# A Hymba-style layer on one core: weight-sum stores, out-projection loads and the first loads put on other queues, and four token rows of the prompt split behind a weight block

## The chip, the cores and the metric

The kernel runs on one core of a Trainium2 chip. The metric is the device time of one launch in microseconds (us); lower is better. 0.2% of the time before is 4.2 us.

## The reference

One encoder layer, called for two inputs that share all weights: a prompt of 512 tokens and a sample of 1024 tokens, model width 2048. All values are fp32.

```
h = rms_norm(x, norm_g)
z = h @ w_in                                  # 2048 -> 5632
c_val, c_glu, c_gate, q, k, v, a_gate = split(z)
conv = conformer_conv(c_val, c_glu, ...)      # sigmoid gate, 31-tap depthwise conv, layer norm, silu, @ w_pw
att  = banded_sink_attention(rope(q), rope(k), v, sink)   # 8 heads, 2 kv heads, window 128
mix  = concat(conv * silu(c_gate), att * silu(a_gate)) @ w_out
y    = rms_norm(x + mix, final_norm_g)
```

## The kernel before

**Products.** TensorE (PE) multiplies in a rounded fp32 form (`fp32r`), so every fp32 operand is split into a high part `hi` and the remainder `lo`, and a product is three matmuls: hi·hi, hi·lo and lo·hi. The split is `parts()` (line 510): ACT writes `hi` with a Copy, DVE writes `lo = x - hi`. Token rows are split by the same function with the norm gain as scale (lines 514 and 515). A token row `t1_n` is 128 model channels by 512 tokens; a weight tile `hl_n` holds both parts of a block.

**Units.** The sample's in- and out-projection run in a seven-product block scheme (class `Unit`): a unit covers a 2x2 grid of weight blocks, and its seven products P1, P2, P6, P5, P7, P3, P4 have 12 matmuls of 128x128 by 128x512 each (line 207). The weights of a unit come as two raw tiles `r1` and `r2` (loads in lines 123 and 127, ring of 3 raw tiles), from which `make0` to `make3` build the split weight tiles `hl` (ring of 3). `make1` forms the differences of blocks that P5, P6 and P4 need, and `less2` the one of P7 (line 143). In the out-projection of the sample (`w_out`), where `sums` is set, these four differences of a unit are also stored to DRAM as `wsum_P..`, because the prompt's out-projection uses them again: 16 units with 4 stores of 256 KB each, made of 512 rows of 512 bytes. The stores are made by `e.store` (line 504), that is, on SyncE's queue (SP).

**The out-projection's accumulators.** Units of class `Onto` do the out-projection in two halves of the contraction. The first half, `over[0]`, starts each of the four output quarters of a unit from the residual `xT_s`, and stores the partial results as `part_out..`; the second half, `over[1]`, starts from `part_out..` and writes the result `y_d`. A quarter lives in an accumulator tile (`u_n` or `g_n`, rings of four), which `begin()` loads (line 285) and into which DVE adds every product when it is done (line 304). `begin()` is called `ahead` products before the quarter's first product, by default two; `u.ahead = 0` is set for the first two units of the second half. These two run as a pair, product by product in turns, since their weights and tokens (`mix_d`, loaded as `p_n` on SP in line 878 and split into `t1_n`) become ready together. The code order sets the order of each queue, up to what the tile scheduler moves by priority; a queue works strictly in order, and a DMA whose tile is not free or not yet written holds what stands behind it.

**The partial sums of the in-projection.** On GpSimd's queue (POOL) stand the stores of partial in-projection results (`part_q`, `part_conv`, `part_gate`, `part_kv`, line 268) and the loads that add them from DRAM into a tile (line 501, an accumulating DMA). POOL has no DMA in the out-projection.

**The prompt's start.** The prompt's in-projection (matmuls in line 669) begins right behind the last unit of the sample's, called `end`. While `end` runs, the prompt's 16 token rows are loaded and split, four behind each of `end`'s first four products (`end.after[0]` to `end.after[3]`, function `follow`), and the first weight block of the prompt is split behind them. The last four token rows (12 to 15) come in with the two loads `load_two(12)` and `load_two(14)`.

**The head.** SP first loads the norm gain `norm_g`, then the first weight block and the sample's token rows in turns (`first()`, line 1888). PE meanwhile runs 20 dummy matmuls of 128x128 by 128x128 (`warm`, line 559).

Of the kernel before, what the change touches and what calls it, by code (L numbers as in the profile page):

```python
# [7 lines left out]
F32 = mybir.dt.float32  # L8
# [5 lines left out]
P = 128  # L14
D = 2048
ND = D // P
# [17 lines left out]
W = 512  # L34
# [59 lines left out]
class Unit:  # L94
# [50 lines left out]
    def make1(self):  # L145

        if self.late:
            t2 = self.e.G([HALF, P]) if self.side or not self.total else self.e.A([HALF, P], F32)
        else:
            t2 = self.e.PT("p", NP, [HALF, P])  # L150
        r1, r2 = self.r1, self.r2
        self.sub(r1[:, 0], r2[:, 0], r1[:, 0])
        self.sub(t2, r2[:, 1], r1[:, 0])
        self.sub(r1[:, 1], r1[:, 1], t2)
        if self.sums:
            for name, x in (("P5", r1[:, 0]), ("P6", t2), ("P4", r1[:, 1])):
                self.e.store(self.sums[name], x)
        t = self.e.hl_tile()
        for o, x in enumerate((r1[:, 0], t2)):
            self.e.parts(t[:, 0, o], t[:, 1, o], x)  # L160
        return t

    def less2(self):
        self.sub(self.r2[:, 0], self.r2[:, 1], self.r2[:, 0])
        if self.sums:
            self.e.store(self.sums["P7"], self.r2[:, 0])
        self.lessened = True

    def make2(self):
# [261 lines left out]
class Encoder:  # L431
# [74 lines left out]
    def parts(self, hi, lo, x, g=None):  # L506

        nc = self.nc
        if g is None:
            nc.scalar.activation(hi, x, AF.Copy)  # L510
            nc.vector.tensor_tensor(lo, x, hi.bitcast(F32), ALU.subtract)  # L511
            self.low_made = nc.cur_bb.bb.instructions[-1]
        else:
            nc.scalar.activation(hi, x, AF.Identity, scale=g)
            nc.vector.scalar_tensor_tensor(lo, x, g, hi.bitcast(F32), ALU.mult, ALU.subtract)
# [45 lines left out]
    def constants(self):  # L561
        nc, a = self.nc, self.a

        def load(key, shape):
            t = self.const.tile([P] + shape, F32, name="c_" + key)
            nc.sync.dma_start(t, a[key])
            return t

        self.norm_g = load("norm_g", [ND])
        self.ones = self.const.tile([P, P], F32, name="ones")  # L570
        nc.vector.memset(self.ones, 1.0)
        self.ones_r = self.const.tile([P, P], F32R, name="ones_r")
        nc.vector.tensor_copy(self.ones_r, self.ones)
        self.norm_n = self.const.tile([P, ND], F32, name="norm_n")

        def rest():
            self.ident = load("ident", [P])
            self.mask = load("mask", [3 * P])
            self.w_dw = load("w_dw", [NC, TAPS])
            self.b_dw = load("b_dw", [NC])  # L580
            self.w_both = self.const.tile([P, NC, (TAPS + 1) // 2], F32, name="w_both")
            nc.vector.tensor_copy(self.w_both[:, :, TAPS // 2 :], self.w_dw[:, :, TAPS - 1 :])
            nc.vector.tensor_tensor(
                self.w_both[:, :, : TAPS // 2], self.w_dw[:, :, 0 : TAPS - 1 : 2], self.w_dw[:, :, 1 : TAPS - 1 : 2], ALU.add
            )
            self.ln_g = load("conv_ln_g", [NC])
            self.ln_b = load("conv_ln_b", [NC])
            self.sink = load("attn_sink", [HEADS])
            self.fin_g = load("final_norm_g", [ND])
            self.stat = {s: self.const.tile([P, TS // P], F32, name=f"stat{s}") for s in (0, 1)}  # L590

        self.more_constants = rest
# [132 lines left out]
    def spread(self, cols, b=NB, room=None):  # L725

        nc = self.nc
        hi = self.work.tile([P, b], F32R, tag="tinyr", bufs=4, name=self.name("tinyr"))
        lo = self.small(b)
        nc.vector.tensor_copy(hi, cols)  # L730
        nc.vector.tensor_tensor(lo, cols, hi.bitcast(F32), ALU.subtract)
        parts = []
        for part in (hi.bitcast(F32), lo):
            dg = (room or self.U)([b * P], F32R)
            for j in range(b):
                nc.vector.tensor_scalar(dg[:, j * P : (j + 1) * P], self.ident, part[:, j : j + 1], None, ALU.mult)
            parts.append(dg)
        yield S8
        ps = self.PS("s", [b * P])
        for n, dg in enumerate(parts):  # L740
            nc.tensor.matmul(ps, self.ones_r, dg, start=n == 0, stop=n == 1)
        return ps
# [1115 lines left out]
def encoder(ctx, tc, a):  # L1858
    e = Encoder(ctx, tc, a)
    sample, prompt = Sequence(e, 0), Sequence(e, 1)  # L1860
# [24 lines left out]

    def first():
        x = [e.F([TS]) for _ in range(NF)] + [e.A([TS], F32)]
        part = lambda k, t: e.nc.sync.dma_start(x[k][:, t * W : t * W + W], sample.xT[k][:, t * W : t * W + W])
        plain.begin()
        for k in range(2 * HALF):  # L1890
            half, j = divmod(k, HALF)
            if j == 0:
                plain.load_some(0, half, 0, 1)
            part(k, 0)
            if j == 0:
                plain.load_some(1, half, 0, 1)
                plain.load_some(0, half, 1)
            if j == 1:
                plain.load_some(1, half, 1)
        for k in range(2 * HALF):  # L1900
            part(k, 1)
        e.loaded = 2
        e.w_load(3)
        e.warm(20, True)
        sums = sample.first_sums(x)
        x = None
        for half in range(2):
            for j in range(HALF):
                if j == 0:
                    plain.make_some(0, half, 0, 1)  # L1910
                next(sums)
                if j < 2:
                    plain.make_some(1 - j, half, j, HALF if j else 1)
                if j == 1:
                    plain.make_some(1, half, 1)
        e.nc.vector.tensor_scalar(e.norm_n, e.norm_g, -1.0, None, ALU.mult)
        for k in range(2 * HALF):
            next(sums)
        e.ready = 2
        plain.after[3] = [lambda: next(sums)]  # L1920
        plain.after[5] = [lambda: e.T.pop("A21")]
        second = stages[0][2]
        for step in (0, 2, 3):
            second.after.setdefault(step, []).append(lambda: next(sums, None))
        second.after[4] = [e.more_constants]
        second.after.setdefault(6, []).append(lambda: setattr(e, "calm", False))

    for u in stages[0][1:3]:
        u.order = TURNS
    plain.before.append(first)  # L1930

    def switch(unit, nxt, g, seq):
# [58 lines left out]
    def load_two(j):  # L1991
        if 8 <= j < 12:
            for i in (0, 1):
                xp[j + i] = e.PT("p", NP, [W])
                e.nc.sync.dma_start(xp[j + i], prompt.xr_d[j // 2][:, i])
            return
        t = e.A([2, TP], F32)
        e.nc.sync.dma_start(t, prompt.xr_d[j // 2])
        xp[j], xp[j + 1] = t[:, 0], t[:, 1]

    def follow(step):
        for k in range(4 * step, 4 * step + 4):
            prompt.split(k, xp.pop(k))
        if step == 0:
            load_two(12)
            load_two(14)
# [6 lines left out]
    end = stages[3][-1]  # L2013
    end.look = NHL - 1
    end.before.append(last_before)
    for step in range(4):
        end.after[step] = [lambda step=step: follow(step)]

    pj = prompt.jobs()
    pj[0].behind = pj[0].early = True  # L2020
# [65 lines left out]
        u.next = v  # L2086
    jobs += grouped(over[0], None) + grouped(over[1], e.A)
    for u in over[1][:2]:
        u.ahead = 0
    over[1][0].next = None  # L2090
    fj[-1].before.append(lambda: chain[0].begin((0, 0)))

# [67 lines left out]
```

## Time and profile before

| | |
|---|---|
| Time, 3 runs | median 2084.76 us (2084.57 to 2086.94) |
| Profiled execution | 2080.18 us, of it 2078.4 us span |
| Granted PE clock, mean | 0.997 of full speed |
| PE busy | 2060.7 us (99%), 9259 matmuls |
| DVE busy | 1754.4 us (84%) |
| ACT busy | 1043.6 us (50%) |
| POOL busy | 122.6 us (6%) |
| DMA | 494.55 MB, mean 238 GB/s |

PE is busy for 99% of the span, so what can change is what lies in the rest: the places where PE waits, and those where its clock was granted only in part. Times within the profile are counted from the start of the span. A row of the timeline gives the start, the time until the last of its instructions ends, the engine (SPq, ACTq and POOLq are a queue's DMA issues), the line, the operation, its tiles, the count, and in brackets how long the engine stood idle before and for what.

### The profile page before, as it was taken

The page shows a single profiled execution, that of the slowest core. Times are in us where ns is not written, and L with a number is a line of the kernel's source. Part 1 is how long each engine was busy: PE and PEld are TensorE (multiplying, and loading weights), DVE is VectorE, ACT ScalarE, POOL GpSimd, SP SyncE. Part 2 cuts the span into 40 slices and gives each one's busy share as a digit, 9 for nine tenths or more (in the row PEclk, how much of TensorE's full clock was granted, in tenths as well). Part 3 has the DMA queues.
Part 4 walks back from the last instruction along what each step waited for, and adds up shares of the span by engine and source line. Part 5 has one row for each costly group of instructions (what it writes and reads, how often), then busy time and mean ns, then how long its engine had stood idle before and what let it go on. Part 6 is the DMA issues. An engine that isn't in the chain of part 4 may idle for free.

```text
span 2078.4 us, 27092 instructions
## 1 busy us (share of the span) xinstructions
PE 2060.7 (99%) x9259; PEld 1699.2 (82%) x9259; DVE 1754.4 (84%) x2873; ACT 1043.6 (50%) x1711; POOL 122.6 (6%) x176
## 2 busy tenths in 40 slices
PE   9999999999999999999999999999999999999998
PEld 8888888888888888788888888888888887888886
DVE  8767899998899999999666877767799977998887
ACT  7485445333464434554455777336454343454454
POOL 0111111111111111100000000000000000000000
PEclk9999999999999999999999999999999999999999
DMA  8888886864577767954455555996789899678897
GB/s 288 312 298 256 199 223 221 285 220 160 188 242 192 175 169 183 280 166 156 153 172 187 177 182 183 315 330 234 247 289 300 278 299 293 220 247 298 289 333 277
DMA packets 245819, 494.55 MB, mean 238 GB/s; under 512 B 23600, under 2 KB 84400, under 8 KB 245680
## 3 DMA queue, kind: packets, MB, share of 16 engines
q1 hardware_dynamic: 225136, 445.62, 63.9%
q0 software_dynamic: 19392, 45.10, 9.4%
q10 hardware_dynamic: 1152, 2.10, 0.3%
q8 instruction: 72, 1.18, 0.2%
q14 instruction: 67, 0.55, 0.1%
HBM read 331.77 MB, written 160.96 MB: 237 GB/s over the span
## 4 chain that ended last, share of the span: by engine, by line
PE 48%; DVE 7%; issue 6%; DMA 4%; ACT 2%; POOL 1%; SPq 0%; ACTq 0%; POOLq 0%; DVEq 0%
PE a L669 13%; PE a L207 7%; PE c L669 6%; PE b L669 6%; PE c L207 3%; PE pv L1196 2%; PE a L1835 2%; PE s L1167 2%; PE s L1835 2%; PE b L207 1%; PE pt L1201 1%; DVE hl L511 1%; DVE f L1003 1%; DVE t L511 1%; DVE f L1040 1%
## 5 line engine op out<-in xcount | busy, mean ns | idle before, releaser
L207 PE MATMUL a<-t,hl 128*128 128x512 f32 x2640 | 633.6, 391 | 4.7 <-DVE u L304 3.2
L207 PEld LDWEIGHTS a<-t,hl 128*128 128x128 f32 x2640 | 494.7, 188 | 110.6 <-DVE u L304 3.6
L510 ACT ACTIVATE hl<-raw 128x1024 fp32r<-128x1024 f32 (+3 forms) x334 | 296.1, 890 | 384.5 <-PE c L207 81.6
L511 DVE TENSOR_TENSOR hl<-raw,hl 128x1024 fp32r<-128x1024 f32 (+3 forms) x334 | 338.8, 1015 | 145.8 <-ACT hl L510 144.4
L669 PE MATMUL a<-t,hl 128*128 128x512 f32 x1344 | 328.0, 394 | 0.0
L207 PE MATMUL c<-t,hl 128*128 128x512 f32 x1320 | 319.2, 389 | 0.0
L207 PEld LDWEIGHTS c<-t,hl 128*128 128x128 f32 x1320 | 247.3, 188 | 51.6 <-DVE u L304 0.4
L669 PEld LDWEIGHTS a<-t,hl 128*128 128x128 f32 x1344 | 248.6, 188 | 49.8
L1040 DVE SCALAR_TENSOR_TENSOR f<-f,c_w_dw,f 128x512 f32<-128x512 f32 x248 | 173.9, 750 | 0.3
L669 PE MATMUL b<-t,hl 128*128 128x512 f32 x672 | 164.6, 395 | 2.2 <-DVE hl L511 2.2
L1003 DVE SCALAR_TENSOR_TENSOR f<-f,c_w_dw,f 128x512 f32<-128x512 f32 x232 | 163.7, 748 | 1.2 <-ACT f L998 1.2
L669 PE MATMUL c<-t,hl 128*128 128x512 f32 x672 | 164.2, 393 | 0.3 <-DVE hl L511 0.3
L207 PE MATMUL b<-t,hl 128*128 128x512 f32 x660 | 160.0, 389 | 0.0
L669 PEld LDWEIGHTS b<-t,hl 128*128 128x128 f32 x672 | 126.1, 190 | 28.0 <-DVE hl L511 2.6
L669 PEld LDWEIGHTS c<-t,hl 128*128 128x128 f32 x672 | 124.7, 188 | 25.5 <-DVE hl L511 0.7
L207 PEld LDWEIGHTS b<-t,hl 128*128 128x128 f32 x660 | 123.7, 188 | 25.6
L1032 DVE SCALAR_TENSOR_TENSOR f<-f,w_both,f 128x512 f32<-128x512 f32 x120 | 90.0, 750 | 2.1
L236 ACT ACTIVATE u<-a 128x512 f32<-128x512 f32 x82 | 48.7, 594 | 66.8 <-PE a L207 64.2
L236 ACT ACTIVATE g<-a 128x512 f32<-128x512 f32 x78 | 46.3, 594 | 69.1 <-PE a L207 64.6
L1181 ACT ACTIVATE p<-p,tiny 128x384 f32<-128x384 f32 (+1 forms) x96 | 54.5, 570 | 39.8 <-DVE tiny L1178 27.3
L510 ACT ACTIVATE a<-pt 128x512 fp32r<-128x512 f32 x64 | 37.9, 593 | 66.3 <-PE pt L1201 66.2
L511 DVE TENSOR_TENSOR a<-pt,a 128x512 fp32r<-128x512 f32 x64 | 44.1, 689 | 27.3 <-ACT a L510 26.6
(350 smaller groups left out, 2687.9 us busy)
## 6 DMA issues: line engine op xcount, KB each, us to landing
raw<-w_in SPq DMA_DIRECT2D x170, 512.0 KB, 5.3
raw<-w_out SPq DMA_DIRECT2D x31, 512.0 KB, 5.0
raw<-w_pw SPq DMA_DIRECT2D x24, 512.0 KB, 4.2
wsum_P<-raw SPq DMA_DIRECT2D x47, 256.0 KB, 3.3
raw<-wsum_P SPq DMA_DIRECT2D x18, 512.0 KB, 5.0
f<-x_s SPq DMA_DIRECT2D x16, 512.0 KB, 8.2
g<-wsum_P SPq DMA_DIRECT2D x28, 256.0 KB, 4.2
a<-sum_S SPq DMA_DIRECT2D x24, 256.0 KB, 6.2
```

What stands on the lines that cost most here:

```text
L207: nc.tensor.matmul(acc, hl[:, l, o, j, :], toks[j][:, r], start=name in FRESH and j == 0 and q == 0, stop=name in LAST and j == HALF - 1 a ...
L236: nc.scalar.activation(t, bank, AF.Copy)
L510: nc.scalar.activation(hi, x, AF.Copy)
L511: nc.vector.tensor_tensor(lo, x, hi.bitcast(F32), ALU.subtract)
L669: nc.tensor.matmul(job.acc[0], hl[:, l, kk // HALF, kk % HALF, :], r, start=i == 0 and p == 0, stop=i == nk - 1 and p == 2,)
L1003: nc.vector.scalar_tensor_tensor(t, h[:, j : j + T], w(j), t, ALU.mult, ALU.add)
L1032: nc.vector.scalar_tensor_tensor(m0, odd[:, j : j + H], both(j), m0, ALU.mult, ALU.add)
L1040: nc.vector.scalar_tensor_tensor(out, d[:, j : j + H], w(2 * j + k), out if j else m0, ALU.mult, ALU.add)
L1167: nc.tensor.matmul(ps[:, 0:n], qs[:, x, h], k[y][:, keys], start=p == 0, stop=p == 2)
L1181: nc.scalar.activation(p[:, 0:n], p[:, 0:n], AF.Exp, bias=nm[:, h : h + 1], accum_out=l[:, h : h + 1])
L1196: nc.tensor.matmul(pv, v[x][:, vs], pt[:, y], start=i == 0 and p == 0, stop=i == last and p == 2)
L1835: nc.tensor.matmul(acc[t], self.toks[name, m][:, x, i, t * P : (t + 1) * P], parts[i][l].rearrange("p a b -> p (a b)"), start=fresh and fi ...
```

## The change

Four edits, each at a queue or an order; the arithmetic stays.

1. The `wsum_P..` stores of `make1` and `less2` go to POOL's queue instead of SP's.
2. The first two units of the second half of the out-projection call `begin()` one product ahead instead of none.
3. In the head, the first half of token row 0 and the norm gain are loaded on ACT's queue, in this order and ahead of all else on ACT; SP starts with the weights. The dummy matmuls go from 20 to 13.
4. The split of the prompt's token rows 12 to 15 goes from `end`'s fourth product to its last one, and is told to be issued behind the `hi` and the `lo` half of what `parts()` made last, which is the prompt's first weight block.

```diff
@@ make1
-                self.e.store(self.sums[name], x)
+                self.e.nc.gpsimd.dma_start(self.sums[name], x)
@@ less2
-            self.e.store(self.sums["P7"], self.r2[:, 0])
+            self.e.nc.gpsimd.dma_start(self.sums["P7"], self.r2[:, 0])
@@ parts
             nc.scalar.activation(hi, x, AF.Copy)
+            self.high_made = nc.cur_bb.bb.instructions[-1]
@@ constants
-        self.norm_g = load("norm_g", [ND])
+        self.norm_g = self.const.tile([P, ND], F32, name="c_norm_g")
@@ first
-        part = lambda k, t: e.nc.sync.dma_start(...)
+        part = lambda k, t, q=e.nc.sync: q.dma_start(...)
         plain.begin()
+        part(0, 0, e.nc.scalar)
+        e.nc.scalar.dma_start(e.norm_g, a["norm_g"])
...
-            part(k, 0)
+            if k:
+                part(k, 0)
...
-        e.warm(20, True)
+        e.warm(13, True)
@@ encoder
-    for step in range(4):
+    def follow_last():
+        with e.tc.issue_after(e.high_made), e.tc.issue_after(e.low_made):
+            follow(3)
+
+    for step in range(3):
         end.after[step] = [lambda step=step: follow(step)]
+    end.after[6] = [follow_last]
...
     for u in over[1][:2]:
-        u.ahead = 0
+        u.ahead = 1
```

**SP at the out-projection's pair, before.** `u_2170` and `g_2180` are the accumulators of the first quarter of the pair's two units, `part_out0_00` and `part_out2_00` what they start from; `a_2161` is `r2` of the pair's second unit, and `p_2166` to `p_2169` are tokens.

```order
L127 DMA a_2161_14931<-w_out 128x1024
L878 DMA p_2166_14954<-mix_d_4_198 128x512
L504 DMA wsum_P6_0_260<-a_2182_15027 128x4x128
L504 DMA part_out14_10_447<-g_2159_14922 128x512
L504 DMA wsum_P4_0_264<-raw_2121_14762 128x4x128
L504 DMA wsum_P5_0_258<-raw_2135_14822 128x4x128
L878 DMA p_2167_14955<-mix_d_5_199 128x512
L504 DMA wsum_P7_0_262<-a_2161_14931 128x4x128
L878 DMA p_2168_14956<-mix_d_6_200 128x512
L878 DMA p_2169_14957<-mix_d_7_201 128x512
L285 DMA u_2170_14962<-part_out0_00_417 128x512
L285 DMA g_2180_15019<-part_out2_00_421 128x512
```

The same queue now, first where the accumulators' loads stand:

```order
L285 DMA u_2170_14955<-part_out0_00_416 128x512
L504 DMA part_out12_01_441<-g_2108_14633 128x512
L285 DMA u_2191_15079<-part_out0_01_417 128x512
L285 DMA g_2159_14915<-xT_s 128x512
L285 DMA g_2180_15012<-part_out2_00_420 128x512
L504 DMA part_out12_10_442<-g_2116_14704 128x512
L123 DMA raw_2135_14815<-w_out 128x1024
L879 DMA p_2140_14838<-msum_0_S1_0_226 128x512
```

and then where the second unit's `r2` stands:

```order
L879 DMA p_2166_14947<-mix_d_4_198 128x512
L879 DMA p_2167_14948<-mix_d_5_199 128x512
L504 DMA part_out14_01_445<-g_2130_14786 128x512
L879 DMA p_2168_14949<-mix_d_6_200 128x512
L285 DMA u_2196_15114<-part_out0_11_419 128x512
L504 DMA part_out14_10_446<-g_2159_14915 128x512
L879 DMA p_2169_14950<-mix_d_7_201 128x512
L285 DMA u_2207_15224<-part_out0_10_418 128x512
L127 DMA a_2161_14924<-w_out 128x1024
```

The loads of `u_2170` and `g_2180` moved from behind four `wsum` stores and four token loads to ahead of the raw tile `raw_2135` and of all these tokens; the load of `a_2161` moved from ahead of the four token loads to behind them.

**DVE at the prompt's first weight block, before.** `hl_961` is that block, `t1_953` to `t1_956` are the token rows 12 to 15, and `g_939`, `u_931`, `g_957` and `c_951` belong to the last results of `end`.

```order
L974 TENSOR_TENSOR g_939_7414<-g_939_7414,f_210_1742 128x512
L515 SCALAR_TENSOR_TENSOR t1_950_7473<-p_929_7374,c_norm_g_278,t1_950_7473 128x512
L974 TENSOR_TENSOR u_931_7380<-u_931_7380,f_210_1742 128x512
L257 TENSOR_TENSOR u_952_7480<-c_951_7476,u_952_7480 128x512
L511 TENSOR_TENSOR hl_961_7552<-raw_921_7347,hl_961_7552 128x1024
L1040 SCALAR_TENSOR_TENSOR f_868_6872<-f_820_6465,c_w_dw_980,f_868_6872 128x512
L515 SCALAR_TENSOR_TENSOR t1_953_7495<-a_936_7406,c_norm_g_278,t1_953_7495 128x512
L515 SCALAR_TENSOR_TENSOR t1_954_7498<-a_936_7406,c_norm_g_278,t1_954_7498 128x512
```

DVE there now, where the block is called `hl_957` and the rows `t1_958` to `t1_961`:

```order
L975 TENSOR_TENSOR g_939_7407<-g_939_7407,f_210_1735 128x512
L516 SCALAR_TENSOR_TENSOR t1_950_7466<-p_929_7367,c_norm_g_278,t1_950_7466 128x512
L975 TENSOR_TENSOR u_931_7373<-u_931_7373,f_210_1735 128x512
L257 TENSOR_TENSOR u_952_7473<-c_951_7469,u_952_7473 128x512
L512 TENSOR_TENSOR hl_957_7533<-raw_921_7340,hl_957_7533 128x1024
L1041 SCALAR_TENSOR_TENSOR f_868_6865<-f_820_6458,c_w_dw_973,f_868_6865 128x512 x4
L420 TENSOR_TENSOR hl_965_7576<-raw_964_7574,hl_965_7576 128x512
L516 SCALAR_TENSOR_TENSOR t1_958_7548<-a_936_7399,c_norm_g_278,t1_958_7548 128x512
```

The five instructions up to the block's `lo` half stand in the same order as before; behind it, three conv taps (line 1041) and `hl_965` moved ahead of the token rows.

**ACT at the same place, before.** `hl_961` is multiplied by token rows 0 to 7, `hl_946` by rows 8 to 15 right behind it.

```order
L514 ACTIVATE t1_953_7495<-a_936_7406,c_norm_g_278 128x512
L514 ACTIVATE t1_954_7498<-a_936_7406,c_norm_g_278 128x512
L514 ACTIVATE t1_955_7501<-a_937_7408,c_norm_g_278 128x512
L510 ACTIVATE hl_961_7552<-raw_921_7347 128x1024
L982 ACTIVATE u_931_7380<-u_931_7380 128x512
L982 ACTIVATE g_939_7414<-g_939_7414 128x512
L983 DMA gate_d0_4_92<-u_931_7380 128x512
L983 DMA gate_d0_6_94<-g_939_7414 128x512
L418 ACTIVATE hl_946_7449<-a_945_7447 128x1024
```

ACT there now, from the first block's `hi` half to the second block's:

```order
L510 ACTIVATE hl_957_7533<-raw_921_7340 128x1024
L983 ACTIVATE g_939_7407<-g_939_7407 128x512
L983 ACTIVATE u_931_7373<-u_931_7373 128x512
L984 DMA gate_d0_6_94<-g_939_7407 128x512
L984 DMA gate_d0_4_92<-u_931_7373 128x512
L236 ACTIVATE g_973_7589<-a_930_7369 128x512
L418 ACTIVATE hl_965_7576<-raw_964_7574 128x1024
L515 ACTIVATE t1_958_7548<-a_936_7399,c_norm_g_278 128x512
L515 ACTIVATE t1_959_7551<-a_936_7399,c_norm_g_278 128x512
L515 ACTIVATE t1_960_7554<-a_937_7401,c_norm_g_278 128x512
L515 ACTIVATE t1_961_7557<-a_937_7401,c_norm_g_278 128x512
L418 ACTIVATE hl_946_7442<-a_945_7440 128x1024
```

The `hi` half of the first block moved ahead of the token rows; the second block's `hi` half moved behind `g_973`, `hl_965` and all four of these rows.

More of the change, by code (lines that the diff above doesn't have):

```diff
@@ L1887, in first @@
         x = [e.F([TS]) for _ in range(NF)] + [e.A([TS], F32)]
-        part = lambda k, t: e.nc.sync.dma_start(x[k][:, t * W : t * W + W], sample.xT[k][:, t * W : t * W + W])
+        part = lambda k, t, q=e.nc.sync: q.dma_start(x[k][:, t * W : t * W + W], sample.xT[k][:, t * W : t * W + W])
         plain.begin()
+        part(0, 0, e.nc.scalar)
+        e.nc.scalar.dma_start(e.norm_g, a["norm_g"])
         for k in range(2 * HALF):
```

## The prediction

> **What bounds the kernel now.** The page comes first: PE is busy for 99% of the span, so a gain has to come from a place where PE waits or runs at a reduced clock. The view of waits, for PE, names these places; each row gives what PE waited for, the sum, the count and the longest.
>
> ```profile
> PE 2060.7 (99%) x9259; PEld 1699.2 (82%) x9259; DVE 1754.4 (84%) x2873; ACT 1043.6 (50%) x1711; POOL 122.6 (6%) x176
> PE a L207 <- DVE u L304: 3.2, 1, 3.2
> PE b L669 <- DVE hl L511: 2.2, 1, 2.2
> PE pt L559 <- DVE ones_r L573: 1.3, 1, 1.3
> PE a L207 <- ACT g L236: 1.1, 1, 1.1
> ```
>
> The first is at the out-projection's pair, the second at the prompt's first weight block, the third at the start; the change touches all three. The fourth lies elsewhere and stays. I read the first in the timelines of PE, DVE and SP.
>
> ```profile
> 1721.97 2.88 PE L207 MATMUL c<-t,hl 128*128 128x512 f32 x12
> 1724.69 1.75 PE L207 MATMUL pt<-t,hl 128*128 128x512 f32 x7
> 1729.67 4.43 PE L207 MATMUL a<-t,hl 128*128 128x512 f32 x12 [3.23 <-DVE u L304]
> 1733.89 3.12 PE L207 MATMUL s<-t,hl 128*128 128x512 f32 x12
> 1736.85 1.30 PE L207 MATMUL pt<-t,hl 128*128 128x512 f32 x5
> 1728.92 0.69 DVE L304 TENSOR_TENSOR u<-a,u 128x512 f32<-128x512 f32 x1 [2.85 <-DMA u<-part_out]
> 1717.61 0.38 SPq L504 DMA_DIRECT2D wsum_P<-a  x1
> 1718.81 1.57 SPq L504 DMA_DIRECT2D wsum_P<-raw  x2
> 1721.22 0.39 SPq L504 DMA_DIRECT2D wsum_P<-a  x1
> 1721.67 1.75 SPq L878 DMA_DIRECT2D p<-mix_d  x2
> 1723.46 0.43 SPq L285 DMA_DIRECT2D u<-part_out  x1
> ```
>
> PE stops because the bank `a` is still full: DVE adds it into the accumulator `u_2170` only at 1728.92, having waited 2.85 for that accumulator's load, which SP issued at 1723.46, behind four `wsum` stores and two token loads. What it costs: from a product's start to the next is 2.72 us in the steady state (1724.69 - 1721.97). The seven matmuls begun at 1724.69 should take 7/12 of that, 1.59; the next begin 4.98 later, so 3.39 is lost. The twelve of the product begun at 1729.67 then take 4.22 (1733.89 - 1729.67) instead of 2.72, and the next twelve 2.96: another 1.50 and 0.24. Together **5.13 us**. The window rows show the second part as clock (columns: busy time of PE, PEld, DVE, ACT, POOL with counts, granted clock, DMA share, GB/s), and another at the second place:
>
> ```profile
> 1730.00:1735.00 5.00, 5.00 (x16) 3.96 (x15) 4.50 (x8) 1.44 (x2) 0.00 (x0) 0.66 0.79 259
> 860.00:865.00 5.00, 5.00 (x16) 3.92 (x16) 4.01 (x7) 1.81 (x3) 0.88 (x1) 0.66 1.02 264
> ```
>
> **Out-projection: stores to POOL, loads earlier (edits 1 and 2).** With `ahead` at 1, the accumulator's load now stands ahead of the last raw tile and of all the pair's tokens on SP, and none of the four stores is ahead of it. Its landing takes 4.4 us:
>
> ```profile
> u<-part_out SPq DMA_DIRECT2D x16, 256.0 KB, 4.4
> a<-w_out SPq DMA_DIRECT2D x1, 512.0 KB, 3.7
> 1715.24 0.33 SPq L127 DMA_DIRECT2D a<-w_out  x1
> 1719.30 0.69 DVE L143 TENSOR_TENSOR raw<-a,raw 128x512 f32<-128x512 f32 x1
> ```
>
> The raw tile and some ten token loads that stood ahead of `a_2161` stand behind it now; at 0.43 us an issue it goes out at 1715.24 - 10 x 0.43 = 1710.9 or earlier, over 10 us ahead of now, and DVE no longer waits for it. The stall of 5.13 goes. What is late next is the second unit's `r2`, the 512 KB load `a_2161`: it was issued at 1715.24 and first used at 1719.30, and now stands behind four token loads and an accumulator load. Five issues of 0.43 would put it 2.2 us later, but the issues ahead of it have become fewer by the stores; I estimate its issue at 1715.3 to 1716.5 and, 3.7 later, its landing at 1719.0 to 1720.2. P6 stands ahead of P5 in both units now, and the second unit's P6 takes the place of the product begun at 1724.69; between landing and that lie four or five DVE instructions of 0.69, some 3 us, so about 1.7 us are to spare. I take 0 for it, and up to 4 as a rival below. Own effect: **-5.0**, bounds -5.1 and -1.
>
> By the Trainium skill ("DMA: Bandwidth & Descriptors", section "Issuing engines are not separate DMA queues") all issuing engines share the same 16 DMA engines, and spreading issues saves only the sequencer's time. By that rule moving the stores alone would give back the 0.38, 1.57 and 0.39 us of issue, 2.3 of the 3.39, and the earlier place on SP would have to bring the rest; no run here shows it yet.
>
> **What the stores cost on POOL.** POOL has had no store of this form. The nearest rows are its own plain stores and its accumulating loads; the third row is the same store on SP, issue to landing.
>
> ```profile
> L268 POOL DMA_DIRECT2D part_q<-u x16 | 8.6, 540 | 68.4 <-DVE u L257 61.8 <-ACT u L236 6.6
> L501 POOL DMA_DIRECT2D g<-part_q x16 | 15.1, 943 | 64.0 <-DVE g L257 55.8 <-PE a L207 8.3
> wsum_P<-raw SPq DMA_DIRECT2D x47, 256.0 KB, 3.3
> 1608.25 0.33 SPq L127 DMA_DIRECT2D raw<-w_out  x1
> 1623.44 0.68 DVE L143 TENSOR_TENSOR raw<-raw,raw 128x512 f32<-128x512 f32 x1
> raw<-w_out SPq DMA_DIRECT2D x31, 512.0 KB, 5.0
> ```
>
> A plain store takes POOL 0.54 us for 128 rows. The `wsum` store has four times the rows, so between 0.54 and 4 x 0.54 = 2.2 us; I take 2.2. A unit lasts 7 x 2.72 = 19.04 us and has four, so POOL is the bound only above 4.76 us each. Below that, a later store only frees a raw tile later: the load at 1608.25 took 5.0 of the 15.2 us before its first use at 1623.44, so 10 us are to spare. I take **0**, bounds 0 and, if stores go one after another at over 4.76, a loss that is a rival below. A gain outside the pair is excluded by the list of waits, which shows no other PE wait in the out-projection.
>
> **The head (edit 3).**
>
> ```profile
> 1.32 4.53 PE L559 MATMUL pt<-ones_r 128*128 128x128 f32 x20 [1.32 <-DVE ones_r L573]
> 5.65 0.73 PE L349 MATMUL a<-t,hl 128*128 128x512 f32 x1
> 0.74 1.28 ACT L510 ACT_TABLE_LOAD   x1 [0.74 <-PEq L2151]
> 4.67 0.72 ACT L514 ACTIVATE t<-f,c_norm_g 128x512 fp32r<-128x512 f32 x1 [1.15 <-DMA f<-xT_s]
> 1.66 0.42 SPq L1888 DMA_DIRECT2D f<-xT_s  x1
> 9.70 1.12 PE L349 MATMUL a<-t,hl 128*128 128x512 f32 x2
> ```
>
> The first token row was issued at 1.66 and used at 4.67, 3.0 us later. On ACT it is issued at 0.74, so it lands near 3.75. The norm gain follows at about 1.2 and the table load is pushed to 1.65 to 2.93, in time. ACT splits the row from 3.75 to 4.45, and the first real matmul starts near 4.55 instead of 5.65. The dummies take at most 4.53 / 20 = 0.23 us each, so thirteen end by 4.3, ahead of it. The matmuls that follow wait for further rows: the second row's load moves up by two issues on SP, 0.42 each, 0.8 in all. So of 1.1 some is lost: **-0.8**, bounds -0.3 and -1.1. At 9.70 two matmuls still take 1.12 us, where twelve take 2.88 in the steady state: the slow stretch at the start lasts to here.
>
> By the Trainium skill ("TensorE: Matmul & The Clock Gate", section "What's actually happening") the clock is raised after a busy window of about 3.4 us that runs freely. By that rule an earlier start could end the slow stretch one window sooner, or the 0.3 us between the last dummy and the first real matmul could end it one later. The rows agree in size: the slow product after 1729.67 and its successor lost 1.74 us, half of 3.4.
>
> **The prompt's first weight block (edit 4).** The timelines of PE, DVE, ACT and POOL:
>
> ```profile
> 856.68 0.61 PE L669 MATMUL b<-t,hl 128*128 128x512 f32 x2
> 859.49 12.36 PE L669 MATMUL b<-t,hl 128*128 128x512 f32 x46 [2.19 <-DVE hl L511]
> 855.74 0.69 DVE L974 TENSOR_TENSOR g<-g,f 128x512 f32<-128x512 f32 x1 [1.00 <-DMA g<-part_gate]
> 858.21 1.22 DVE L511 TENSOR_TENSOR hl<-raw,hl 128x1024 fp32r<-128x1024 f32 x1
> 855.46 1.04 ACT L510 ACTIVATE hl<-raw 128x1024 fp32r<-128x1024 f32 x1
> 846.72 0.88 POOL L501 DMA_DIRECT2D g<-part_gate  x1 [4.91 <-DVE g L257]
> ```
>
> The third matmul needs the block's `lo` half, which DVE makes from 858.21 to 859.43. ACT had the `hi` half ready at 856.50. DVE was held before that: it waited 1.00 for the accumulating load of `g_939`, issued by POOL at 846.72, and then had four instructions in order, `g_939`, `t1_950`, `u_931` and `u_952`, ahead of the `lo` half. The change brings the `hi` half forward by about 1.5 us, but these four still stand ahead of it in DVE's order. So the `lo` half begins at 858.2 as before, and the stall of 2.19, with the reduced clock behind it, stays: **0**. The token rows 12 to 15 come later on both engines: on DVE behind four conv taps and a weight half, so from 859.4 + 5 x 0.69 = 862.9, and four of 0.69 make them by 865.6. They are needed from the block's 37th matmul, twelve of 0.227 (2.72 / 12) ahead of the end of the 46 near 871.8: 869.1. The second block's `hi` half, `hl_946`, now stands on ACT behind the four rows, and is needed from the 25th matmul, by the same count at 866.4. The last gate activation can begin when DVE has `u_931`, by 858.2; with 0.72 for each of 512 columns (the row of the head) and 1.04 for 1024, one gate activation, `g_973`, `hl_965`, four rows and `hl_946` make 6 x 0.72 + 2 x 1.04 = 6.4, so 864.6. Both are in time, the second by under 2 us. Bounds: -3.9 (2.19 and, for the reduced clock, the pair's 1.74) if the `lo` half does come forward, +1.5 if `hl_946` is late.
>
> **Sum.** -5.0 - 0.8 = -5.8 against the profiled execution, 2080.18 to 2074.4. That execution lies 4.58 under the median of the runs, and I take the change off the median: 2084.76 - 5.8 = **2079.0**.
>
> **Rivals.**
> *r2 late* (17%). The token loads ahead of `a_2161` wait for tiles; if it lands 2 to 4 us later than put, PE stalls at the second unit's P6 instead, with the clock loss behind it. For it speaks that four loads now stand ahead; against it the 1.7 us to spare. Gain 1.3 to 3.3: 2081.5 to 2083.5.
> *More goes* (9%). The `lo` half at the prompt comes forward too, -3.9 more, or the slow stretch at the head ends sooner, by as much as the pair's slow stretch cost, 1.50 + 0.24 = 1.74: 2075.1 to 2077.3. DVE's unchanged order speaks against the first.
> *POOL can't keep up* (13%), the slower side. If a store holds POOL until it has landed and that takes more than the 3.3 of SP's row, the point is 4.76 us each. At 5.4, each unit falls behind by 4 x 5.4 - 19.04 = 2.56 us; over 16 units 41, less the 10 to spare: +31, so 2110. A store just at the edge costs a late raw tile or two, +5 to +10: 2084 to 2089. Against it, POOL is otherwise idle there and the row of 0.94 us for an accumulating load is far below.
> *No change that counts* (6%). The prompt's second block comes late (+1.5) or the head's slow stretch lasts longer by the same 1.74, while the pair gains half: 2083 to 2086.
> The forecast itself has 55%, with its own range 2076.5 to 2080.8.
>
> **Chances.** A measurement of this kernel tells 0.2%, 4.2 us, from no change: faster is under 2080.6, slower over 2088.9. Faster: 51 of the forecast's 55, and the 9 of the second rival: 0.60. Same: the rest of the forecast, the late `r2`, the no-change case and half of POOL's edge cases: 0.30. Slower: the rest of POOL, 0.10. Range 2075 to 2086: it leaves out POOL's bad case and a little at the low end.
>
> **What would show it.** Right: in the profile after, no wait of PE for line 304, no window at 0.66 in the pair, the accumulator's load issued before 1712, `hl` (line 511) still waited for about 2.2 us at the prompt, the first real matmul near 4.5. Wrong: a PE wait for a weight part (line 511 or 510) at the pair's second P6; `wsum` rows of over 4.7 us on POOL with SP waiting for raw tiles; the prompt's wait gone.

## The result, and the profile after

The changed kernel takes **2119.51 us** (median of 5 runs, 2115.08 to 2125.35) against 2084.76 for the kernel before (5 runs, 2084.21 to 2086.94): ratio **1.0168**, 95% interval 1.0149 to 1.0187. It is slower by 35 us where 5.8 us less were forecast. The profiled execution is the longest of the five, 2125.35 us, so its waits are somewhat above the typical ones.

The page's first rows and the view of waits for PE and for SP, of the changed kernel:

```profile
span 2123.6 us, 27178 instructions
PE 2072.4 (98%) x9252; PEld 1702.9 (80%) x9252; DVE 1752.0 (83%) x2873; ACT 1043.3 (49%) x1711; POOL 170.2 (8%) x240
PE a L207 <- DVE u L304: 11.9, 3, 8.9
PE c L207 <- DVE u L304: 5.9, 2, 3.6
PE a L207 <- ACT hl L510: 4.5, 1, 4.5
PE pv L1197 <- DVE a L512: 3.7, 1, 3.7
PE b L670 <- DVE hl L512: 3.0, 1, 3.0
SPq L127 <- DMA wsum_P<-raw: 60.9, 13, 7.8
SPq L285 <- DMA wsum_P<-g: 32.9, 8, 7.5
```

Where before had one wait of 3.2 us in the whole out-projection, there are now several up to 8.9. Between the two profiled executions the span grows by 45.2 us. In 33.5 of them PE stands idle; for the other 11.7 it is busy longer with the same products, at a mean granted clock of 0.992 instead of 0.997. The last two rows name the place: SP stood 94 us (122 with two smaller rows of the kind) before loads of raw tiles (line 127) and accumulators (line 285), because their tiles were still being read by a `wsum` store. In SP's waits of before there are three such rows, 10.6 us in all; this is the largest:

```profile
SPq L127 <- DMA wsum_P<-raw: 8.5, 5, 2.9
```

The timeline of POOL over one unit and a bit shows why. Each row is the issue of one store:

```profile
1584.04 0.75 POOL L157 DMA_DIRECT2D wsum_P<-raw  x1 [7.44 <-DVE raw L143]
1588.74 0.76 POOL L157 DMA_DIRECT2D wsum_P<-g  x1 [3.95 <-DVE tiny L1179]
1595.00 0.75 POOL L157 DMA_DIRECT2D wsum_P<-raw  x1 [5.49 <-issue]
1599.99 0.76 POOL L166 DMA_DIRECT2D wsum_P<-raw  x1 [4.24 <-issue]
1609.91 0.75 POOL L157 DMA_DIRECT2D wsum_P<-raw  x1 [9.16 <-DVE raw L143]
wsum_P<-raw POOLq DMA_DIRECT2D x47, 256.0 KB, 4.4
```

POOL is busy for only 0.76 us with a store, but the four of a unit start 4.70, 6.26 and 4.99 us apart, while one takes 4.4 us from issue to landing (last row, the median). Two of the four show "issue", that is, nothing in the trace that they waited for. The landing of each store, read singly from the trace, tells what it was: the first three land 4.40, 5.95 and 4.69 us after their start, and each time the next store starts 0.30 us after that. None of the 64 stores starts before the one ahead of it has landed, and 49 of the 63 that have one ahead start within 0.37 us of its landing. So the last of the four starts 15.95 us after the first, and the tiles that they read come free late.

How this reaches PE is best seen at the longest wait (timelines of SP, ACT, DVE and PE):

```profile
1723.63 0.32 SPq L285 DMA_DIRECT2D g<-part_out  x1
1726.47 0.33 SPq L123 DMA_DIRECT2D raw<-w_out  x1
1726.89 2.23 SPq L879 DMA_DIRECT2D p<-msum_S  x4
1731.85 0.63 ACT L510 ACTIVATE t<-p 128x512 fp32r<-128x512 f32 x1 [11.34 <-DMA p<-msum_S]
1735.49 1.23 DVE L512 TENSOR_TENSOR hl<-raw,hl 128x1024 fp32r<-128x1024 f32 x1 [9.37 <-ACT hl L510]
1737.24 0.68 DVE L304 TENSOR_TENSOR u<-a,u 128x512 f32<-128x512 f32 x1
1738.07 7.17 PE L207 MATMUL a<-t,hl 128*128 128x512 f32 x24 [8.87 <-DVE u L304]
```

SP issues in order, and four token loads (`p<-msum_S`) stood behind the accumulator and raw-tile loads that waited for tiles. ACT waited 11.34 us for these tokens, DVE 9.37 for ACT's weight half, the accumulator addition stands on DVE behind that half, and PE waited 8.87 for the bank. The pair's own place, 20 us later, no longer has the old wait.

### The profile page after: what moved, and what is told of

Same layout as the page of the kernel before. It is cut to its first block, busy times and chain, and to the rows that moved or that the text cites. A ratio compares the mean times of both kernels' runs of the same rounds, so it can differ in the third digit from the quotient of the medians.

```text
span 2123.6 us, 27178 instructions
## 1 busy us (share of the span) xinstructions
PE 2072.4 (98%) x9252; PEld 1702.9 (80%) x9252; DVE 1752.0 (83%) x2873; ACT 1043.3 (49%) x1711; POOL 170.2 (8%) x240
## 3 DMA queue, kind: packets, MB, share of 16 engines
q10 hardware_dynamic: 1440, 2.37, 0.3%
## 4 chain that ended last, share of the span: by engine, by line
PE 32%; issue 17%; DVE 10%; DMA 6%; POOL 2%; ACT 1%; SPq 0%; POOLq 0%; DVEq 0%; ACTq 0%
PE a L670 12%; PE b L670 6%; PE c L670 5%; DVE hl L512 2%; PE pv L1197 2%; PE a L1836 2%; PE s L1168 2%; POOL wsum_P L157 1%; DMA a<-ag_d 1%; PE pt L1202 1%; PE s L1836 1%; DMA raw<-w_in 1%; DVE f L1033 1%; DMA g<-gate_d 1%; DVE f L1004 1%
## 5 line engine op out<-in xcount | busy, mean ns | idle before, releaser
L157 POOL DMA_DIRECT2D wsum_P<-raw x32 | 24.3, 758 | 854.0 <-DMA f<-msum_S 672.7
```

What stands on the lines that cost most here:

```text
L157: self.e.nc.gpsimd.dma_start(self.sums[name], x)
```

## The experiments

Twelve kernels were run, four at a time. The kernel before, run with them, had medians of 2086.42, 2085.72 and 2086.19 us and single runs from 2081.08 to 2091.89, so differences of 2 us can be told only by the interval of the ratio, if at all.

**1. The stores back on SP** (edit 1 undone, the rest kept):

```diff
-                self.e.nc.gpsimd.dma_start(self.sums[name], x)
+                self.e.store(self.sums[name], x)
...
-            self.e.nc.gpsimd.dma_start(self.sums["P7"], self.r2[:, 0])
+            self.e.store(self.sums["P7"], self.r2[:, 0])
```

> The changed kernel with the four wsum stores of a unit back on SP (edit 1 undone, edits 2 to 4 kept). Theory A (on POOL each wsum store starts only when the one before has landed, about 5 us, and four of them exceed a unit's 19.04 us; raw tiles and accumulators come free late and SP stands behind them): the loss of 35 us is gone, the time is 2080 to 2086, no PE wait for line 304 over 1 us outside the pair. Theory B (the earlier accumulator loads of edit 2 hold SP): the loss stays, 2105 or more.

Measured: 2086.90 us, ratio 1.0003 (0.9993 to 1.0014). The whole loss is gone: it was edit 1's. The pair's wait of PE is back, at 3.1 us, though `ahead` is 1 here. With the stores on SP the accumulator's load is still issued behind them, at 1729.87:

```profile
1728.20 0.36 SPq L504 DMA_DIRECT2D wsum_P<-a  x1
1728.61 1.22 SPq L879 DMA_DIRECT2D p<-mix_d  x2
1729.87 0.44 SPq L285 DMA_DIRECT2D u<-part_out  x1
1736.33 4.60 PE L207 MATMUL a<-t,hl 128*128 128x512 f32 x12 [3.11 <-DVE u L304]
```

So edit 2 without edit 1 does nothing for this wait; edit 1 is what brought the load forward. The code says why: the first quarter of a unit is begun by the unit before it or by `open()` (lines 298 and 289 of the kernel before), whatever `ahead` is. `ahead` moves only the loads of the later quarters.

**2. The stores on POOL alone** (the kernel before with edit 1).

> The kernel before with edit 1 alone (wsum stores on POOL). Theory A: 2110 to 2122, the stores on POOL 4 to 6 us apart when they queue, SP waiting for their landing. Theory B: 2082 to 2088.

Measured: 2119.83 us, ratio 1.0166 (1.0152 to 1.0181), the same as the whole change. Theory B, that edit 2's earlier loads hold SP, is ruled out as the cause of the loss.

**3. A little more room for POOL's descriptors**, in the changed kernel:

```diff
-    nc = bacc.Bacc("TRN2", ..., dynamic_dma_scratch_size=1024)
+    nc = bacc.Bacc("TRN2", ..., dynamic_dma_scratch_size=1152)
```

> The changed kernel with one number changed: dynamic_dma_scratch_size 1152 instead of 1024, the SBUF room in which POOL's DMAs keep their descriptors. A store of 512 rows is 32 rows for each of 16 DMA engines; if the room of 1024 holds 64 descriptors and a store takes 33, one fits, and in 1152 (72) two. Theory A1 (POOL waits for room for descriptors): stores no longer wait for the one before, most of the 35 us is gone, 2080 to 2092. Theory A2 (POOL's stores are serial for another reason, or the transfers themselves are slow): as changed, 2112 to 2125.

Measured: 2086.02 us, ratio 0.9998 (0.9988 to 1.0007). One number, 128 bytes, takes away the 33 us. The instructions stand in the same order on every engine as in the changed kernel, so it is not the schedule. The stores now overlap:

```profile
1584.34 0.75 POOL L157 DMA_DIRECT2D wsum_P<-raw  x1 [14.73 <-DVE raw L143]
1586.71 0.76 POOL L157 DMA_DIRECT2D wsum_P<-g  x1 [1.62 <-DVE g L143]
1590.16 0.75 POOL L157 DMA_DIRECT2D wsum_P<-raw  x1 [2.69 <-DVE raw L143]
1591.55 0.75 POOL L166 DMA_DIRECT2D wsum_P<-raw  x1 [0.64 <-DVE f L941]
1605.83 0.75 POOL L157 DMA_DIRECT2D wsum_P<-raw  x1 [13.53 <-DVE raw L143]
wsum_P<-raw POOLq DMA_DIRECT2D x47, 256.0 KB, 4.2
```

First to last is 7.2 us instead of 15.95, with the same 0.75 us of POOL for each and nearly the same landing (4.2 for 4.4). The next unit follows 21.5 us after this one instead of 25.9. So neither POOL's work nor the transfer is slow; in the changed kernel each store waited for the one before to land. Now two are under way: the second starts 2.37 us after the first, which lands 5.5 us after its start, and the third and the fourth start 0.31 us after the landing of the first and of the second. Of all 64 stores none starts before the last but one has landed, while 48 of 63 start before the last one has.

**4. Three stores on POOL, P7 on SP** (only the second line of edit 1 undone).

> The changed kernel with only the P7 store of each unit back on SP, so that POOL has three stores per unit. Theory A: 3 x 5 = 15 us is under a unit's 19.04, so the backlog does not grow from unit to unit; most of the loss is gone, 2083 to 2097. Theory B or a loss from slower transfers for each store moved: three quarters of the loss stay, 2108 to 2114.

Measured: 2097.98 us, ratio 1.0058 (1.0043 to 1.0073): a third of the loss is left, just above the expected 2097. With one store in four gone, two thirds of the loss are, so it is not a price per store. But three spaced stores still free the tiles late, so it isn't only whether POOL keeps up over a unit; SP's waits have

```profile
SPq L285 <- DMA wsum_P<-g: 34.2, 8, 9.1
```

**5. Each store as two halves**, in the changed kernel, room 1024:

```diff
-                self.e.nc.gpsimd.dma_start(self.sums[name], x)
+                for h in (0, HALF // 2):
+                    self.e.nc.gpsimd.dma_start(self.sums[name][:, h : h + HALF // 2], x[:, h : h + HALF // 2])
```

(and the same for P7).

> The changed kernel (room for descriptors 1024 as there) with each wsum store made as two DMAs of half the rows (256 rows of 512 bytes each). Theory A1 (room for descriptors): a half takes 17 of the 64, three fit, so the next store's first half starts while the last half is under way; most of the loss goes, 2083 to 2097. Theory A3 (POOL runs one DMA after another whatever its size): twice as many landings to wait for, slower than the changed kernel, over 2125.

Measured: 2094.14 us, ratio 1.0043 (1.0030 to 1.0056). Twice as many DMAs with the same bytes and rows are 25 us faster than the changed kernel. That rules out that POOL runs one DMA after another whatever its size. Here three are under way: none of the 128 halves starts before the third ahead of it has landed, and 58 start 0.31 us after that landing. A half has half the rows and half the bytes, so this run alone does not tell which of them counts. The kernel before does, with the same room of 1024: its 172 DMAs on POOL also move 256 KB each, but in 128 rows, and 95 of them start before the one ahead has landed. So what counts is how many rows are under way.

**6. Edits 1 and 2 alone, room 1152** (from the kernel before).

> The kernel before with edits 1 and 2 alone and the room for descriptors at 1152. The pair's wait of 3.2 is gone with its slow stretch and nothing else of before moves: 3 to 5 us under before, ratio 0.9976 to 0.9990. If the ratio is 1.000, something in the out-projection gives it back (late r2, SP behind stores), and the profile shows a PE wait there.

Measured: 2087.47 us, ratio 1.0011 (1.0002 to 1.0021). The expected gain did not come. The pair's wait is gone, but two others of the same kind are there, 2.7 us in sum, the longer just ahead of the pair:

```profile
PE a L207 <- DVE u L304: 2.7, 2, 2.1
1711.36 1.96 ACT L510 ACTIVATE t<-p 128x512 fp32r<-128x512 f32 x3 [4.03 <-DMA p<-msum_S]
1714.30 1.23 DVE L511 TENSOR_TENSOR hl<-raw,hl 128x1024 fp32r<-128x1024 f32 x1 [3.77 <-ACT hl L510]
1716.87 7.29 PE L207 MATMUL a<-t,hl 128*128 128x512 f32 x24 [2.06 <-DVE u L304]
SPq L285 <- DMA wsum_P<-g: 2.4, 1, 2.4
```

It is the chain of the changed kernel's longest wait in small: tokens late on SP, then ACT, then a weight half on DVE ahead of the accumulator addition. The last row is from SP's waits between 1690 and 1712: ahead of these tokens SP stands 2.4 us before an accumulator's load, because a `wsum` store on POOL still reads the tile. The kernel before has no such wait in that stretch.

**7. Edit 4 alone.**

> The kernel before with edit 4 alone. As forecast: the PE wait for the prompt's first weight block (line 511/512) stays at 2.2, no change, ratio 0.9995 to 1.0005. If edit 4 costs what e1 and the changed kernel show around there (a wait of 3.0, and 1.3 us near 1380), ratio 1.0005 to 1.0015.

Measured: 2085.18 us, ratio 1.0002 (0.9993 to 1.0011); no change, as forecast. The wait at the prompt's first weight block:

```profile
PE b L670 <- DVE hl L512: 1.8, 1, 1.8
```

**8. Edit 3 alone.**

> The kernel before with edit 3 alone. The first real matmul at 5.4 as in the changed kernel, because the split of token row 0 waits for the norm gain, which lands behind the row on ACT's queue; gain 0 to 0.3, not to be told by the time, ratio 0.9995 to 1.0005.

Measured: 2086.93 us, ratio 1.0006 (0.9996 to 1.0016). No gain that the time shows.

**9. Edit 1 alone, room 1152**, `ahead` left at 0.

> The kernel before with edit 1 alone and the room for descriptors at 1152 (ahead stays 0). The kernel with edit 2 beside these gained 5 us at the pair and lost 4 one unit earlier, where ACT waited for tokens and a raw tile that stood on SP behind the pair's accumulator loads. Theory C (edit 2's early loads hold SP): without them the tokens and the raw tile are in time, no PE wait near 1712, the pair's wait is left at 0 to 2; ratio 0.998 to 1.000. Theory D (POOL's stores free the tiles late, whatever stands on SP): the loss one unit earlier stays, ratio 1.000 to 1.002.

Measured: 2087.05 us, ratio 1.0004 (0.9994 to 1.0015). Theory C as written fails: the waits for line 304 are still there, the longer again just ahead of the pair, and the pair's first accumulator load is issued as early with `ahead` at 0:

```profile
PE a L207 <- DVE u L304: 2.0, 2, 1.5
1695.05 0.45 SPq L285 DMA_DIRECT2D u<-part_out  x1
```

Once the stores are off SP, then, the schedule moves it forward by itself, and the loss in experiment 6 does not come from edit 2. The time and the wait are as Theory D had them, and SP stands 2.5 us for a tile that a `wsum` store on POOL still reads, as in experiment 6. That speaks for D, but no run separates it from the rest.

**10. The accumulators' loads on POOL instead of the stores** (from the kernel before; the stores stay on SP, `ahead` is 1 for the pair):

```diff
     def begin(self, n):
         if n not in self.d:
             self.d[n] = self.e.E()
-            self.e.nc.sync.dma_start(self.d[n], self.source(*n))
+            (self.e.nc.gpsimd if self.total else self.e.nc.sync).dma_start(self.d[n], self.source(*n))
```

> The kernel before with its wsum stores left on SP, ahead at 1 for the pair, and the accumulator loads of the second half of the out-projection (begin, line 285) issued on POOL, which has nothing else there; rows of 2 KB, 128 to a load. Theory C: nothing on SP stands behind these loads any more and they stand behind no store, so the pair's 5.1 us goes and nothing is late one unit earlier: ratio 0.9970 to 0.9985 (3 to 6 us). If the pair was held by something else, ratio 0.999 to 1.001.

Measured: **2082.89 us, ratio 0.9985** (0.9977 to 0.9994), faster than both kernels. The load that the pair waited for is issued by POOL at 1690.45, and PE runs through the pair with two short waits for weights:

```profile
1690.45 0.58 POOL L285 DMA_DIRECT2D u<-part_out  x1 [824.34 <-DMA p<-mix_d]
1725.13 2.89 PE L207 MATMUL s<-t,hl 128*128 128x512 f32 x12
1727.86 0.63 PE L207 MATMUL a<-t,hl 128*128 128x512 f32 x2
1728.80 2.56 PE L207 MATMUL a<-t,hl 128*128 128x512 f32 x10 [0.30 <-DVE hl L511]
1731.26 0.73 PE L207 MATMUL s<-t,hl 128*128 128x512 f32 x2
1732.40 2.57 PE L207 MATMUL s<-t,hl 128*128 128x512 f32 x10 [0.41 <-DVE hl L511]
1734.81 2.88 PE L207 MATMUL c<-t,hl 128*128 128x512 f32 x12
```

The two products from 1727.86 to 1734.81 take 6.95 us instead of 2 x 2.72 = 5.44, so 1.5 of the 5.1 us is left; 3.6 is gained there, and the time is 3.3 us lower.

**11. Room for 68 descriptors instead of 64**: the changed kernel with 1088.

> The changed kernel with the room for descriptors at 1088 (68 for each DMA engine) instead of 1024. If a store takes 33, two fit in 68 as in 72: 2082 to 2090, as with 1152. If it takes 34 or more, or room comes in larger steps, only one fits: 2110 to 2125.

Measured: 2086.44 us, ratio 1.0002 (0.9993 to 1.0011), as with 1152. The point lies between 1024 and 1088 bytes. At 16 bytes each that is between 64 and 68, so two stores fit in 68 and not in 64: 33 or 34 for a store of 32 rows per DMA engine. The halves of experiment 5 agree: 17 each lets three into 64 and not four. That one descriptor has 16 bytes, and that the rows are shared evenly by 16 DMA engines, was taken as given, not measured.

**12. Experiment 10 with edit 4, and the tasks behind the sample's last in-projection unit two products later** (`end.landing = LANDING + 2`).

> As the kernel with the accumulator loads on POOL, and edit 4, and the tasks that use the accumulated results of the sample's last in-projection unit put off by two more products (landing 6 instead of 4 for that unit), so that on DVE the first of them no longer stands ahead of the prompt's first weight block. If DVE's order holds PE there, as the prediction had it: PE's wait for line 511/512 at the prompt is under 1 us instead of 2.2 with no slow stretch, 2 to 4 us beyond the kernel with the loads on POOL, ratio 0.9950 to 0.9980. If the wait stays, something else is late (ACT, the weight's load).

Measured: 2083.89 us, ratio 0.9988 (0.9979 to 0.9996), not told apart from experiment 10. The prompt's wait moved instead of going:

```profile
860.79 5.30 PE L670 MATMUL b<-t,hl 128*128 128x512 f32 x22 [0.48 <-DVE hl L512]
865.10 1.06 ACT L418 ACTIVATE hl<-raw 128x1024 fp32r<-128x1024 f32 x1 [4.34 <-DMA raw<-w_in]
867.90 1.04 ACT L418 ACTIVATE hl<-a 128x1024 fp32r<-128x1024 f32 x1
869.00 3.26 PE L670 MATMUL b<-t,hl 128*128 128x512 f32 x13 [2.91 <-ACT hl L418]
```

The first block's `lo` half now costs 0.48 us, so it was DVE's order that held PE there: the addition into `g_939`, which in the kernel before stood ahead of that half and waited 1.00 for its load, has gone behind it. But PE then waits 2.91 for the second block's `hi` half (the ACT row at 867.90). Edit 4 put it on ACT behind `hl_965` and the token rows, and in this run ACT waits 4.34 for the raw tile of `hl_965` first. With edit 4 alone that wait is 0.70, and PE does not wait for the second block.

## Why the prediction was wrong

**POOL (edit 1): the step that failed.** The prediction took 0 for the stores on POOL, from a price of at most 2.2 us of POOL's time and 10 us to spare for the tiles. POOL's time was even smaller, 0.76. What the sum left out is that a store could not start until the one before had landed (0.30 us after it, 49 times of 63). It named this as a rival at 13% ("if a store holds POOL until it has landed"), with the point at 4.76 us each and 2110 for a bad case; the spacing came out at 4.7 to 6.3 and the time at 2119.5. The rival's mechanism held, but its working did not quite: POOL did not fall behind steadily, since it stood idle for 7 to 9 us before the first store of each of the two units shown. The late release of the tiles itself made the next unit late (25.9 us a unit instead of 21.5), so the loss grew already with three stores. The row that should have warned was the third of that part, 3.3 us from issue to landing, close enough to 4.76 to matter if nothing overlaps; the two rows taken as nearest, with 128 rows to a DMA, could not show a limit on rows.

**The pair (edits 1 and 2): mechanism right, net wrong.** Its stall went, as said, and not through edit 2 (experiments 1 and 9). In the changed kernel the late release brought larger waits elsewhere. With that cured (experiments 3, 6 and 9) the ratio is 0.9998 to 1.0011 and not 0.998: a part of the gain is given back just ahead of the pair, on the same kind of accumulator addition. In the working the step "over 10 us ahead of now, and DVE no longer waits" asked what the load is behind, and not who is behind the loads and the late tiles on SP. Moving the loads off SP and leaving the stores there gives the gain (experiment 10). That tiles still come free late is seen in SP's waits (2.4 and 2.5 us in experiments 6 and 9). How much of what is given back comes from them, and how much from the schedule's new order on DVE, stays open.

The rule of the Trainium skill ("DMA: Bandwidth & Descriptors", section "Issuing engines are not separate DMA queues") is that issuing on another engine saves only the sequencer's time. From it the prediction worked out that moving the stores alone would give back 2.3 of the 3.39 us. The runs differ from that in both directions. In experiment 9, with the stores alone moved and room for two of them, the load is issued at 1695.05 instead of 1723.46 and the pair's wait for line 304 is gone: the load's place in SP's order moved, and not only an issue's time. That the new queue can have a limit of its own, the rule does not say, and that decided the case.

**The head (edit 3): too large.** -0.8 was forecast; the first real matmul starts at 5.41 instead of 5.65:

```profile
1.17 0.46 ACTq L1892 DMA_DIRECT2D c_norm_g<-norm_g  x1
f<-xT_s ACTq DMA_DIRECT2D x1, 256.0 KB, 3.4
c_norm_g<-norm_g ACTq DMA_DIRECT2D x1, 8.0 KB, 3.4
4.57 0.17 DVE L1920 TENSOR_SCALAR norm_n<-c_norm_g 128x16 f32<-128x16 f32 x1 [3.31 <-DMA c_norm_g<-norm_g]
4.64 0.72 ACT L515 ACTIVATE t<-f,c_norm_g 128x512 fp32r<-128x512 f32 x1 [0.43 <-DMA c_norm_g<-norm_g]
5.41 0.80 PE L349 MATMUL a<-t,hl 128*128 128x512 f32 x1 [1.05 <-ACT t L515]
```

"The norm gain follows at about 1.2, in time" was wrong: issued at 1.17 behind token row 0, its 8 KB landed only at 4.55, 3.4 us later. In the kernel before, first on SP, they take 1.6. The row was late too, at 4.14 where 3.75 was put, but the split of row 0 waited for the gain, not for the row. PE stood idle for 1.05 us after the thirteen dummies.

**The prompt (edit 4): as forecast.** The wait stays, 3.0 us in the changed kernel and 1.8 with edit 4 alone, and the ratio of edit 4 alone is 1.0002. The reason given, DVE's order, is borne out by experiment 12. The margin of under 2 us for `hl_946` is used up there, by a term that the prediction had at nothing: the wait of ACT for the raw tile of `hl_965`, 4.34 us in that run. The reduced clock behind the wait does not always come: the 46 matmuls take 12.36 us before and 10.88 with edit 4 alone, but 10.73 in experiment 2 too, which leaves edit 4 out.

## What to carry to other kernels

Before a DMA is moved to another queue, ask not only what an issue costs there but how many rows of it may be under way at once, and compare the landing time with the spacing that is needed: a store that is over in 0.76 us for its engine held the next one until it had landed, some 5 us later. On a queue that works in order, move the short loads that others wait for, and leave the stores that nothing waits for at once where they are; moving the loads gained 3.3 us here, while moving the stores lost 35 with room for one of them and gained nothing that the time shows with room for two. And of a load that is brought forward, ask who now stands behind it.

## What the runs showed of the hardware

The room for descriptors of POOL's DMAs sets how many rows can be under way: with 1024 bytes one store of 512 rows of 512 bytes or three of 256 rows, with 1088 two of 512, a difference of 33 us in the time. The next store starts 0.30 to 0.31 us after the landing that makes room for it. The trace does not name the wait; it shows as idle time of POOL ahead of the store, put down to whatever ended last or to "issue".

The 8 KB of the norm gain took 3.4 us to land behind 256 KB on ACT's queue, 0.4 us after these, against 1.6 us as the first load on SP. SP's first weight loads were under way at the same time, so how much of it is the place in the queue is not shown.
